# Norm statistics from token-major x in the weight stream, and four PSUM banks for the stream's sums

## The chip, the cores and the metric

The kernel runs on one core of one Trainium2 chip. A core has TensorE (PE, matrix products into PSUM), VectorE (DVE), ScalarE (ACT), GpSimd (POOL) and SyncE (SP), whose queue issues the DMAs here. PSUM has eight banks of 128 x 512 fp32 in this kernel's use. The metric is device time in microseconds (us), the median of several runs; lower is better.

## The reference

A hybrid block over x of 256 tokens and 2048 channels: a root-mean-square norm, one wide input projection, three mixers (A: state space, B: attention with selected, window and compressed keys, C: retention), a gated merge, an output projection and a gated embedding.

```python
def rms_norm(x, gain=None):
    y = x * lax.rsqrt(jnp.mean(x * x, axis=-1, keepdims=True) + EPS)
    return y * gain
...
    h = rms_norm(x, norm_pre[i])
    (xa, za, ba, ca, dta, qb, kcb, vcb, ksb, vsb, kwb, vwb, gb, zb,
     qc, kc, vc, zc, gm) = jnp.split(h @ w_in[i], offsets, axis=-1)
    ya = ssd_mixer(xa, za, ba, ca, dta, ...)
    yb = nsa_mixer(qb, kcb, vcb, ksb, vsb, kwb, vwb, gb, zb, ...)
    yc = retention_mixer(qc, kc, vc, zc, ret_norm[i])
    u = jnp.einsum('bsjw,jwd->bsjd', jnp.stack([ya, yb, yc], axis=2), w_branch[i])
    gates = jax.nn.sigmoid(gm).reshape(b, L, N_BRANCH, D_MODEL)
    x = x + rms_norm(jnp.sum(gates * u, axis=2) @ w_out[i], norm_post[i])
    g = jax.nn.sigmoid(rms_norm(x) @ ple_gate[i])
    x = x + rms_norm(g * (p[i] @ ple_proj[i]), ple_norm[i])
```

## The kernel before

All weights pass through one stream. plan (L27) lists its pieces: a chunk is 512 output columns of one weight matrix, such as ba0 or qc0, in four pieces of 1 MB each (four k-tiles of 128 rows by 512 columns). load (L187) issues a piece's DMA on SP into one of three raw buffers; split (L197) makes a high part hi on ACT (L214) and a low part lo on DVE (L215), both in the reduced format fp32r. mm_part then multiplies each k-tile with x, which is held transposed and split in the same way (xh, xl): three products hi.xh, lo.xh, hi.xl (L938, L939, L940) for each of two halves t of the tokens, so 96 matmuls of 128 x 512 a chunk. A "stream matmul" below is one of these, counted from the program's start. Their sums stand in a PSUM bank of the pool mm (mmbank, three banks), one for each chunk and half, until evac reads it. Two more pools are tp (two banks, transposes) and bg (bgbank, three banks, the products of the mixers, called the background here).

x is multiplied with norm_pre but not with its norm: the projections use raw x, and every evacuation scales by rstd, one number for each token. So no bank can be evacuated before rstd is there.

The start is written by hand: first (L234) loads x transposed (xtr, which lies in the tile yh) and the first chunk in fine pieces, and first_split (L244) makes for each k xh on ACT (L248), xl on DVE (L249), hi on ACT (L253) and lo on DVE (L254). stats (L263) squares xtr on ACT (L266, eight of 128 x 512), adds the squares on POOL (L269, seven), sums over the channels with small matmuls against ones (by Chain, L130), and rsqrt (L174) makes rstd. The piece sm (columns for dt and the gates) comes after ba0 and is multiplied in small (L296).

The background of a chunk is written after the chunk (pend, flush, after). For a key/value group g of branch B, bg_q does soft for each half of the tokens (four rounds r: scores into one or two bg banks, L600 and L603; copy L611 on ACT; mask adds L612 and L613 and maximum L616 on DVE; exps L619 on ACT; scaling L624 on DVE), then soft_cmp for the compressed keys (L632 to L652), then mix: tiles of transposes (L181), a high part on ACT (L666, tile u1) and a low part on DVE (L667, tile u2), products with the values (L130), and the copy of the result to y (L671). bg_zb then multiplies with the gate of the chunk zb and writes yh (L487, ACT) and yl (L488, DVE), from which the chunks wB are multiplied. q0 to q3 are the four groups; the chunks run q0, zb0, ... q3, zb3, gmB0, qc0, wB0.

A scheduler that works on a modelled timeline sets the order of the instructions on each engine out of what is ready, data and free buffers both. Each engine then runs its list in that order, so one waiting instruction holds up all behind it.

Of the kernel before, what the change touches and what calls it, by code (L numbers as in the profile page):

```python
# [8 lines left out]
F32 = mybir.dt.float32  # L9
# [5 lines left out]
P = 128  # L15
# [11 lines left out]
def plan():  # L27
    """The weight stream: a list of (chunk, piece); a chunk is (kind, index)."""
    s = []

    def add(kind, n):
        s.extend(((kind, n), j) for j in range(4))

# [5 lines left out]
    for kind, cnt in (("ba", 2), ("ca", 2), ("xa", 4), ("za", 4)):  # L39
        for n in range(cnt):  # L40
            add(kind, n)
            if kind == "ba" and n == 0:
                s.append((("sm", 0), 0))
# [42 lines left out]
def build(ctx, tc, I, out, LA=3, SA=2, HB=4, WARM=9):  # L86
    nc = tc.nc
    ST = plan()
    NP = len(ST)
    SM = ST.index((("sm", 0), 0))  # L90

# [21 lines left out]
    def mmbank():  # L113
        return PS("mm", [P, CH], 3)

# [3 lines left out]
    def bgbank(shape):  # L119
        return PS("bg", shape, 3)  # L120

    nodep = mybir.DependencyInfo(mybir.DependencyClass.NoSync, mybir.DependencyReason.DATA)

    class Chain:
        """Keeps the accumulation groups of one PSUM bank in trace order."""
        def __init__(self):
# [11 lines left out]

# [1 line left out]
    cst = const.tile([P, I["cst"].shape[1]], F32, name="cst")  # L140
# [27 lines left out]
    nc.vector.memset(ones, 1.0)  # L168
    # the activation tables load while the first operands are on their way
    ld = const.tile([P, 1], F32, name="ld")  # L170
    nc.scalar.activation(ld, ones, AF.Copy)

    def rsqrt(dst, src, n):
        """dst = (src / n + eps) ** -0.5"""  # L174
        w = src.shape[-1]
        t = W("rs", [P, w], 2)
        nc.vector.tensor_scalar(t, src, 1.0 / n, EPS, ALU.mult, ALU.add)
        nc.gpsimd.tensor_tensor(out=dst, in0=t, in1=mhalf.to_broadcast([P, w]), op=ALU.pow)
# [3 lines left out]

# [1 line left out]
    raw = {}  # L184
    spl = {}

    def load(s):  # L187
        if ST[s][0][0] == "sm":
            raw[s] = stream.tile([P, KT, 80], F32, name=nm("raw"), tag="raw", bufs=3)
            nc.sync.dma_start(raw[s], I["ws"])  # L190
            return
        raw[s] = stream.tile([P, 4 * CH], F32, name=nm("raw"), tag="raw", bufs=3)
        if s < 4:
            return
        nc.sync.dma_start(raw[s], I["wst"][s if s < SM else s - 1])

    def split(s):  # L197
        if ST[s][0][0] == "sm":
            hi, lo = BIG("mg", [P, 2, KT, 80], F32R), None
            hi, lo = hi[:, 0], hi[:, 1]  # L200
            nc.scalar.activation(hi, raw[s], AF.Copy)
            nc.vector.tensor_sub(lo, raw[s], hi.bitcast(F32))
            spl[s] = (hi, lo)
            del raw[s]
            return
        hs, ls = [], []
        for h in range(2):
# [4 lines left out]
            if s >= 4:  # L212
                r = raw[s][:, h * 2 * CH:(h + 1) * 2 * CH]
                nc.scalar.activation(hi, r, AF.Copy)  # L214
                nc.vector.tensor_sub(lo, r, hi.bitcast(F32))  # L215
# [3 lines left out]

# [1 line left out]
    xh = BIG("xh", [P, KT, T], F32R)  # L221
    xl = BIG("xl", [P, KT, T], F32R)
    xtr = BIG("yh", [P, KT, T])
    xsq = BIG("yl", [P, KT, T])
    ssq = BIG("y", [P, 2, T])

    # keeps the tensor engine busy, and so at its full clock, until the first operands are there
    wz = W("u1", [P, CH], 2, mybir.dt.bfloat16)
# [5 lines left out]
    def first(q):  # L234
        """k-tiles 4q..4q+3 of x and of the first chunk's weights, loaded and split finely"""
        load(q)
# [26 lines left out]
    def stats():  # L263
        """rstd per token from the transposed x, and the tables of scales that hang on it"""
        for k in range(0, KT, 2):
            nc.scalar.activation(xsq[:, k:k + 2, :], xtr[:, k:k + 2, :], AF.Square)  # L266
            if k == 0:
                continue
            nc.gpsimd.tensor_tensor(out=ssq, in0=xsq[:, 0:2, :] if k == 2 else ssq, in1=xsq[:, k:k + 2, :], op=ALU.add)  # L269
        ps = bgbank([P, 2])  # L270
        ch = Chain()
        for t in range(2):
            for i in range(2):
                ch.mm(ps[:, t:t + 1], ssq[:, i, t * P:(t + 1) * P], ones, i == 0, i == 1)
        rsqrt(rstd, ps, D)
        # tables of scales per token for branches B and C
        nc.vector.tensor_scalar_mul(rsc, rstd, 128.0 ** -0.5)
# [5 lines left out]
    rk = [rstd[:, t:t + 1] for t in range(2)]  # L283
# [1 line left out]
    sg = const.tile([P, 2, 48], F32, name="sg")  # L285
# [6 lines left out]
    def small(wsh, wsl):  # L292
# [19 lines left out]
        nc.scalar.activation(ea, V.alog, AF.Exp)  # L312
        # log(1 + e) = 2 atanh(e / (2 + e)), by its series: (e / (2 + e)) ** 2 is at most 1 / 9
        z = W("dtz", [P, 2, 32], 1)
# [21 lines left out]

# [1 line left out]
    S = K()  # L338
# [7 lines left out]
    def to_T(rows, pair):  # L346
        """rows: the tokens' tile per half; pair of 128-column blocks -> PSUM [128, 2, 256]"""
        tp = tpbank([P, 2, T])
# [5 lines left out]

# [1 line left out]
    def conv(rows, ct0, dest):  # L356
# [37 lines left out]
    def bg_xa(n):  # L394
# [20 lines left out]
        nc.gpsimd.tensor_tensor(out=xe, in0=xdt[0], in1=bc(dend[:, hsl]), op=ALU.mult)  # L415
        # the state after the first chunk
        st = bgbank([P, CH])
# [31 lines left out]

# [1 line left out]
    def ev_z(ps, n, t):  # L451
# [51 lines left out]

# [44 lines left out]
    def bg_cmpout(i, ps):  # L548
# [9 lines left out]
        if i == 0:  # L558
# [6 lines left out]
            return  # L565
        # rows 0..15, 16..31 and 32..47: [high, high, low], for [high, low, high] of the other operand
        h3 = W("u4", [P, 2, 4, 3, 16], 2)
# [10 lines left out]
    def bg_q(g):  # L578
# [49 lines left out]
        def soft_cmp(t, ss):  # L628
            sgt = sg[:, t, :].rearrange("p (h b) -> p h b", b=3)
            # compressed keys  # L630
            mx = W("mx", [P, 4], 2)
# [45 lines left out]

# [1 line left out]
    def ev_rot(ps, kind, n, t):  # L679
# [56 lines left out]

# [1 line left out]
    def ev_w(ps, br, n, t):  # L738
# [31 lines left out]

# [1 line left out]
    def ev_wo(ps, n, t):  # L772
# [74 lines left out]
    def ev_pg(ps, n, t, half=None):  # L847
        """half: of the columns of the last chunk, whose last token half comes in two parts"""
        c0, w = (n * CH, CH) if half is None else (n * CH + half * 256, 256)
# [20 lines left out]

# [1 line left out]
    def evac(ch, ps, t):  # L872
# [50 lines left out]

    acc = {}

    def mm_part(ch, j, t, hs, ls, half=None):
        """the products of piece j of a chunk for half t of the tokens (and half of the columns)"""
        H, L = lhs(ch[0])
# [12 lines left out]
        if j == 3:  # L941
            if half is None:
                evac(ch, ps, t)
            else:
                ev_pg(ps, ch[1], t, half)
            del acc[key]
# [15 lines left out]
    for q in range(4):  # L962
        first(q)
    nc.sync.dma_start(cst, I["cst"])
    nc.sync.dma_start(vec, I["vec"])
    done = [4, 4]
    pend = []

    def ahead(s):
        while done[0] <= min(s + LA, NP - 1):  # L970
            load(done[0])
            done[0] += 1
            while done[1] <= min(s + SA, done[0] - 1):
                split(done[1])
                done[1] += 1
        while done[1] <= min(s + SA, NP - 1):
            split(done[1])
            done[1] += 1
# [6 lines left out]
    while s < NP:  # L985
        ch, j = ST[s]
        two = (ch == ("wo", 3) and j == 2) or (ch == ("pg", 0) and j == 0) or (ch == ("pg", 3) and j == 2)
        if s < 4:
            first_split(s)
            if s == 1:  # L990
                stats()
        ahead(s)
        if ch[0] == "cmp":
            flush()
# [20 lines left out]
        del spl[s]  # L1015
        if j == 3:
            pend.append(ch)
        s += 1


# [1 line left out]
CST = [("ident", (P,)), ("tri", (P,)), ("stri", (P,)), ("cos", (2, P)), ("sin", (2, P)),  # L1022
# [37 lines left out]
def layout(inputs):  # L1060
# [9 lines left out]
    def block(w):  # L1070
        """[2048, 512] -> 4 pieces [128, 4 * 512]"""
        return w.reshape(4, 4, P, CH).transpose(0, 2, 1, 3).reshape(4, P, 4 * CH)
# [18 lines left out]
    ST = plan()  # L1091
    ST.remove((("sm", 0), 0))
    wst = np.empty((len(ST), P, 4 * CH), np.float32)
# [47 lines left out]
```

## Time and profile before

| | |
|---|---|
| median of 3 runs | 1828.5 us (1827.67 to 1828.92) |
| span of the profiled execution | 1826.8 us |
| PE busy | 1809.6 us (99%) |
| DVE busy | 1080.0 us (59%) |
| ACT busy | 950.5 us (52%) |
| POOL busy | 176.7 us (10%) |
| bytes moved by DMA | 333.72 MB, 183 GB/s in the mean |

The page gives no time of the profiled execution other than its span. Busy time is the sum over an engine's instructions without overlap. A PE row's duration (about 0.39 us for 128 x 512) is the time from its start to its end, and the next one starts earlier, since matmuls are pipelined; what a matmul costs PE is the step from one start to the next. In a timeline the brackets give the idle time of the engine before an instruction and what ended it.

### The profile page before, as it was taken

The page shows a single profiled execution, that of the slowest core. Times are in us where ns is not written, and L with a number is a line of the kernel's source. Part 1 is how long each engine was busy: PE and PEld are TensorE (multiplying, and loading weights), DVE is VectorE, ACT ScalarE, POOL GpSimd, SP SyncE. Part 2 cuts the span into 40 slices and gives each one's busy share as a digit, 9 for nine tenths or more (in the row PEclk, how much of TensorE's full clock was granted, in tenths as well). Part 3 has the DMA queues.
Part 4 walks back from the last instruction along what each step waited for, and adds up shares of the span by engine and source line. Part 5 has one row for each costly group of instructions (what it writes and reads, how often), then busy time and mean ns, then how long its engine had stood idle before and what let it go on. Part 6 is the DMA issues. An engine that isn't in the chain of part 4 may idle for free.

```text
span 1826.8 us, 21792 instructions
## 1 busy us (share of the span) xinstructions
PE 1809.6 (99%) x8531; PEld 1502.2 (82%) x8531; DVE 1080.0 (59%) x1453; ACT 950.5 (52%) x1264; POOL 176.7 (10%) x167
## 2 busy tenths in 40 slices
PE   8999999999999999999999999999999999999997
PEld 6888888888888888888878888888888888888886
DVE  7666876544457547667674545655656544555665
ACT  6656566544346547656754444344445544444653
POOL 2001340000022000000011011102110000110001
PEclk9999999999999999999999999999999999999999
DMA  7443434555556654344435555445454555565653
GB/s 284 164 182 139 152 141 176 184 192 199 185 183 254 232 194 151 139 161 147 149 144 196 196 186 205 162 165 189 170 207 175 184 188 203 185 230 186 228 185 116
DMA packets 49496, 333.72 MB, mean 183 GB/s; under 512 B 5617, under 2 KB 6385, under 8 KB 10225
## 3 DMA queue, kind: packets, MB, share of 16 engines
q1 hardware_dynamic: 48960, 331.67, 50.3%
q8 instruction: 67, 1.10, 0.2%
q10 hardware_dynamic: 432, 0.66, 0.1%
q14 instruction: 37, 0.30, 0.0%
HBM read 330.21 MB, written 2.10 MB: 182 GB/s over the span
## 4 chain that ended last, share of the span: by engine, by line
PE 95%; ACT 2%; DVE 1%; issue 1%; POOL 0%; DMA 0%; SPq 0%; POOLq 0%; ACTq 0%; DVEq 0%
PE mm L939 28%; PE mm L940 28%; PE mm L938 28%; PE tp L181 3%; PE bg L130 2%; PE bg L137 1%; PE bg L600 1%; PE bg L957 1%; DVE lo L215 0%; PE bg L433 0%; DMA raw<-wst 0%; ACT hi L214 0%; PE mm L844 0%; PE mm L296 0%; POOL u L540 0%
## 5 line engine op out<-in xcount | busy, mean ns | idle before, releaser
L215 DVE TENSOR_TENSOR lo<-raw,hi 128x1024 fp32r<-128x1024 f32 x604 | 745.0, 1237 | 596.0 <-ACT hi L214 573.6
L214 ACT ACTIVATE hi<-raw 128x1024 fp32r<-128x1024 f32 x604 | 637.8, 1060 | 644.0 <-PE mm L940 623.6
L939 PE MATMUL mm<-lo,xh 128*128 128x512 f32 x1856 | 727.0, 393 | 3.6 <-DVE lo L254 3.1
L940 PE MATMUL mm<-hi,xl 128*128 128x512 f32 x1856 | 725.0, 392 | 0.0
L938 PE MATMUL mm<-hi,xh 128*128 128x512 f32 x1856 | 719.9, 392 | 0.5 <-ACT hi L253 0.5
L939 PEld LDWEIGHTS mm<-lo,xh 128*128 128x128 f32 x1856 | 348.9, 188 | 77.3 <-DVE lo L254 6.1
L938 PEld LDWEIGHTS mm<-hi,xh 128*128 128x128 f32 x1856 | 348.3, 188 | 72.1 <-ACT hi L253 1.7
L940 PEld LDWEIGHTS mm<-hi,xl 128*128 128x128 f32 x1856 | 348.8, 188 | 69.8 <-issue 0.2
L939 PE MATMUL mm<-lo,yh 128*128 128x512 f32 x496 | 193.6, 390 | 0.0
L940 PE MATMUL mm<-hi,yl 128*128 128x512 f32 x496 | 193.1, 390 | 0.0
L938 PE MATMUL mm<-hi,yh 128*128 128x512 f32 x496 | 192.6, 390 | 0.0
L940 PEld LDWEIGHTS mm<-hi,yl 128*128 128x128 f32 x496 | 93.1, 188 | 19.2
L938 PEld LDWEIGHTS mm<-hi,yh 128*128 128x128 f32 x496 | 93.1, 188 | 19.2
L939 PEld LDWEIGHTS mm<-lo,yh 128*128 128x128 f32 x496 | 93.1, 188 | 18.9
L748 POOL TENSOR_TENSOR mg<-mg,u 128x512 f32<-128x512 f32 x16 | 27.9, 1745 | 372.0 <-DVE u L747 372.0
L430 POOL TENSOR_TENSOR u<-ahl,cst 128x512 fp32r<-128x512 f32 x32 | 43.5, 1373 | 92.9 <-PE bg L433 62.4
L366 DVE SCALAR_TENSOR_TENSOR u<-tp,vec,u 128x255 f32<-128x255 f32 (+2 forms) x96 | 41.0, 473 | 5.0 <-ACT u L362 4.6
L540 POOL TENSOR_TENSOR u<-gate,vec 128x120 f32<-128x120 f32 x32 | 21.9, 723 | 212.4 <-ACT gate L516 211.2
L647 POOL COPY pc<-pch 128x64 f32<-128x64 f32 x8 | 5.7, 715 | 341.8 <-ACT pch L644 341.8
L619 ACT ACTIVATE u<-u,nmx 128x128 f32<-128x128 f32 (+1 forms) x64 | 28.5, 446 | 6.4 <-DVE nmx L616 2.9
L181 PE MATMUL tp<-cst,u 128*128 128x128 f32 (+1 forms) x194 | 30.1, 273 | 0.8 <-ACT u L368 0.8
L690 POOL TENSOR_TENSOR u<-u,u 128x256 f32<-128x256 f32 x16 | 18.6, 1162 | 112.0 <-DVE u L688 94.6
(236 smaller groups left out, 1208.2 us busy)
## 6 DMA issues: line engine op xcount, KB each, us to landing
raw<-wst SPq DMA_DIRECT2D x302, 1024.0 KB, 4.8
raw<-wst SPq DMA_DIRECT2D x6, 512.0 KB, 8.6
y<-xn SPq DMA_DIRECT2D x2, 1024.0 KB, 5.9
xl<-plen SPq DMA_DIRECT2D x2, 1024.0 KB, 5.0
yh<-xT SPq DMA_DIRECT2D x6, 256.0 KB, 8.5
out_dram<-xh SPq DMA_DIRECT2D x4, 352.0 KB, 2.4
raw<-wst SPq DMA_DIRECT2D x4, 256.0 KB, 4.4
u<-npost SPq DMA_DIRECT2D x4, 256.0 KB, 4.8
```

Of the source, the lines that this page charges most:

```text
L130: i = nc.tensor.matmul(o, lhsT, rhs, start=start, stop=stop)
L181: nc.tensor.transpose(dst, src, ident[0:k, 0:k])
L214: nc.scalar.activation(hi, r, AF.Copy)
L215: nc.vector.tensor_sub(lo, r, hi.bitcast(F32))
L366: nc.vector.scalar_tensor_tensor(cv[:, jj, sh:], tp[:, jj, :T - sh], V.cw[:, ct, j:j + 1], cv[:, jj, sh:], ALU.mult, ALU.add)
L430: nc.gpsimd.tensor_tensor(out=asg, in0=ahl[:, i, c, 4 * g:4 * g + 4].bitcast(F32).unsqueeze(2).to_broadcast([P, 4, P]), in1=CP.tri.unsquee ...
L540: nc.gpsimd.tensor_tensor(out=bf[:, :, g, :], in0=src[:, g], in1=V.pe[:, i, l0:l0 + 8].unsqueeze(2).to_broadcast([P, 8, 15]), op=ALU.add)
L619: nc.scalar.activation(pr_[:, b, :], pr_[:, b, :], AF.Exp, bias=nmx[:, b:b + 1], accum_out=sm2[:, b:b + 1])
L748: nc.gpsimd.tensor_tensor(out=S.mg[:, t, sl], in0=S.mg[:, t, sl], in1=tmp, op=ALU.add)
L938: nc.tensor.matmul(ps, H[:, kk, tsl], wh, start=(kk == 0), stop=False)
L939: nc.tensor.matmul(ps, H[:, kk, tsl], wl, start=False, stop=False)
L940: nc.tensor.matmul(ps, L[:, kk, tsl], wh, start=False, stop=(kk == KT - 1))
```

## The change

- stats no longer uses xtr. Two pieces of token-major x, ("xn", 0) and ("xn", 1), 1 MB each, stand in the stream after the second and third piece of ba1. split squares each on ACT as one 128 x 2048 activation with the sum accumulated into a column of ssx, and after the second one rsqrt makes rstd from ssx. The squares of xtr, the POOL adds and the small matmuls are gone.
- The two sums of ba0 stay in their banks (late) until then; they are evacuated and ba0's background is queued after the second piece.
- The piece sm moves from behind ba0 to behind ba1; its split parts lie in the tile yh.
- mmbank has four banks, bgbank two.
- The two DMAs of the tables cst and vec are issued behind the load of stream piece 4, and ahead (the look-ahead of loads and splits) does not split beyond piece 3 in the first three steps.
- Comments and docstrings are blanked; line numbers shift by 5 to 19, by 10 in mm_part, by 9 in the background.

```diff
     def add(kind, n):
-        s.extend(((kind, n), j) for j in range(4))
+        for j in range(4):
+            s.append(((kind, n), j))
+
+            if (kind, n) == ("ba", 1) and j in (1, 2):
+                s.append((("xn", j - 1), 0))
...
-            if kind == "ba" and n == 0:
+            if kind == "ba" and n == 1:
                 s.append((("sm", 0), 0))
...
     def mmbank():
-        return PS("mm", [P, CH], 3)
+        return PS("mm", [P, CH], 4)
...
     def bgbank(shape):
-        return PS("bg", shape, 3)
+        return PS("bg", shape, 2)
...
     def split(s):
+        if ST[s][0][0] == "xn":
+            t = ST[s][0][1]
+            nc.scalar.activation(xj, raw[s], AF.Square, accum_out=ssx[:, t:t + 1])
+            spl[s] = None
+            del raw[s]
+            if t == 1:
+                stats()
+                for ev in late:
+                    evac(*ev)
+                pend.append(("ba", 0))
+            return
...
     def stats():
-        for k in range(0, KT, 2):
-            nc.scalar.activation(xsq[:, k:k + 2, :], xtr[:, k:k + 2, :], AF.Square)
-            if k == 0:
-                continue
-            nc.gpsimd.tensor_tensor(out=ssq, in0=xsq[:, 0:2, :] if k == 2 else ssq, in1=xsq[:, k:k + 2, :], op=ALU.add)
-        ps = bgbank([P, 2])
-        ch = Chain()
-        for t in range(2):
-            for i in range(2):
-                ch.mm(ps[:, t:t + 1], ssq[:, i, t * P:(t + 1) * P], ones, i == 0, i == 1)
-        rsqrt(rstd, ps, D)
+        rsqrt(rstd, ssx, D)
...
         if j == 3:
-            if half is None:
+            if ch == ("ba", 0):
+                late.append((ch, ps, t))
+            elif half is None:
                 evac(ch, ps, t)
...
-    nc.sync.dma_start(cst, I["cst"])
-    nc.sync.dma_start(vec, I["vec"])
...
             load(done[0])
+            if done[0] == 5:
+                with tc.issue_after(getattr(dma[0], "ins", dma[0])):
+                    nc.sync.dma_start(cst, I["cst"])
+                    nc.sync.dma_start(vec, I["vec"])
             done[0] += 1
-            while done[1] <= min(s + SA, done[0] - 1):
+            while done[1] <= min(s + SA if s > 2 else 3, done[0] - 1):
                 split(done[1])
...
             first_split(s)
-            if s == 1:
-                stats()
```

How the order moves, at three places. First ACT in the start, the rows that follow the table load; xh and hi are the split of x and of the weights, and the tile yl of the row with L266 holds squares. Before:

```order
L248 ACTIVATE xh_80<-yh_82,npre 128x256 [waits DMAHW1_49,DMAHW0_49]
L253 ACTIVATE hi_134<-raw_108 128x512 [waits DMAHW2_49]
L248 ACTIVATE xh_80<-yh_82,npre 128x256 [waits DMAHW3_49]
L266 ACTIVATE yl_83<-yh_82 128x512
L253 ACTIVATE hi_134<-raw_108 128x512 [waits DMAHW4_49]
L248 ACTIVATE xh_80<-yh_82,npre 128x256 [waits DMAHW5_49]
L253 ACTIVATE hi_136<-raw_108 128x512 [waits DMAHW6_49]
L248 ACTIVATE xh_80<-yh_82,npre 128x256 [waits DMAHW7_49]
L266 ACTIVATE yl_83<-yh_82 128x512
```

After:

```order
L267 ACTIVATE xh_80<-yh_82,npre 128x256 [waits DMAHW1_49,DMAHW0_49]
L272 ACTIVATE hi_132<-raw_108 128x512 [waits DMAHW2_49]
L267 ACTIVATE xh_80<-yh_82,npre 128x256 [waits DMAHW3_49]
L272 ACTIVATE hi_132<-raw_108 128x512 [waits DMAHW4_49]
L267 ACTIVATE xh_80<-yh_82,npre 128x256 [waits DMAHW5_49]
L272 ACTIVATE hi_134<-raw_108 128x512 [waits DMAHW6_49]
L267 ACTIVATE xh_80<-yh_82,npre 128x256 [waits DMAHW7_49]
```

The squares have gone, and the splits of x and of the weights follow each other.

Second PE at the border of the chunks gmB0 and qc0, around the first matmul of qc0 (mm_7623 before, mm_7609 after); bg, tp, u and ev belong to the mix of q2 and to the background of zb2. Before:

```order
L938 MATMUL mm_7494<-hi_7513,xh_80 128x512
L939 MATMUL mm_7494<-lo_7514,xh_80 128x512
L940 MATMUL mm_7494<-hi_7513,xl_81 128x512
L938 MATMUL mm_7623<-hi_7543,xh_80 128x512 [waits Activation_49]
L939 MATMUL mm_7623<-lo_7544,xh_80 128x512 [waits DVE_49]
L940 MATMUL mm_7623<-hi_7543,xl_81 128x512
```

After:

```order
L135 MATMUL bg_6672<-u_1244_6714,yl_4735 128x512 [waits Activation_49]
L135 MATMUL bg_6672<-u_1245_6715,yl_4735 128x512 [waits DVE_49]
L135 MATMUL bg_6672<-u_1244_6714,yl_4735 128x512
L135 MATMUL bg_6672<-u_1232_6670,vc_847_4797 128x512
L186 MATMUL tp_6871<-cst,ev_6826 128x128 [waits PE_49]
L186 MATMUL tp_6871<-cst,ev_6840 128x128
L186 MATMUL tp_6871<-cst,ev_6826 128x128
L186 MATMUL tp_6871<-cst,ev_6840 128x128
L948 MATMUL mm_7609<-hi_7529,xh_80 128x512 [waits Activation_49]
```

Before, the first matmul of qc0 follows the last ones of gmB0 directly; after, the second half of q2's mix (33 rows of transposes and products ahead of qc0, of which the last eight are printed) stands between the two chunks.

Third PE around the first matmuls of wB0, which read yh (mm_7779 before, mm_7765 and mm_7778 after); bg rows with u1 and u2 of L130 and L135 are mix products, those of L612 scores of soft, tp rows transposes of the softmaxed scores. Before:

```order
L940 MATMUL mm_7636<-hi_7655,xl_81 128x512
L938 MATMUL mm_7779<-hi_7685,yh_7476 128x512
L939 MATMUL mm_7779<-lo_7686,yh_7476 128x512
L130 MATMUL bg_7271<-u_1361_7289,yl_4749 128x512 [waits Activation_49]
L130 MATMUL bg_7271<-u_1362_7290,yl_4749 128x512 [waits DVE_49]
L130 MATMUL bg_7271<-u_1361_7289,yl_4749 128x512
L181 MATMUL tp_7308<-cst,u_1319_7122 128x128 [waits PE_49]
L181 MATMUL tp_7308<-cst,u_1324_7143 128x128
```

After:

```order
L612 MATMUL bg_7164<-yh_4487,gate_7019 128x256 [waits DVE_49]
L612 MATMUL bg_7164<-yh_4487,gate_7019 128x256
L612 MATMUL bg_7164<-yh_4487,u_1298_7021 128x256
L948 MATMUL mm_7765<-hi_7671,yh_7462 128x512 [waits Activation_49]
L949 MATMUL mm_7765<-lo_7672,yh_7462 128x512
L948 MATMUL mm_7778<-hi_7671,yh_7462 128x512
L949 MATMUL mm_7778<-lo_7672,yh_7462 128x512
L135 MATMUL bg_7207<-u_1345_7213,yl_4735 128x512 [waits DVE_49]
L135 MATMUL bg_7207<-u_1346_7214,yl_4735 128x512
L135 MATMUL bg_7207<-u_1345_7213,yl_4735 128x512
```

Before, the first matmuls of wB0 stand behind q3's second to last mix tiles, with three tiles to go; after, they stand directly behind the last round of q3's soft, with both calls of mix and the second soft_cmp still to go.

## Rows read from the trace of the kernel before

**Rows 1.** The page, part 1: each engine's busy time, share of the span and instructions.

```profile
PE 1809.6 (99%) x8531; PEld 1502.2 (82%) x8531; DVE 1080.0 (59%) x1453; ACT 950.5 (52%) x1264; POOL 176.7 (10%) x167
```

**Rows 2.** Stretches: us, busy PE, PEld, DVE, ACT, POOL (count), PEclk, DMA share, GB/s.

```profile
10.00:20.00 10.00, 7.28 (x28) 4.72 (x28) 9.09 (x11) 9.83 (x22) 6.68 (x5) 1.00 1.03 384
34.61:1817.00 1782.39, 1779.77 (x8419) 1482.03 (x8417) 1048.76 (x1403) 923.13 (x1211) 161.61 (x152) 1.00 0.50 181
887.60:938.35 50.75, 49.72 (x250) 40.60 (x248) 36.31 (x96) 39.12 (x76) 1.91 (x4) 1.00 0.41 147
1820.00:1823.00 3.00, 0.00 (x0) 0.00 (x0) 2.42 (x2) 1.01 (x2) 2.33 (x3) 0.50 0.31 120
```

**Rows 3.** Timeline of PE, start: start, duration, instruction, [idle before, releaser].

```profile
5.14 1.22 PE L938 MATMUL mm<-hi,xh 128*128 128x512 f32 x2
...
10.91 0.74 PE L938 MATMUL mm<-hi,xh 128*128 128x512 f32 x2 [0.46 <-ACT hi L253]
...
25.78 0.50 PE L939 MATMUL mm<-lo,xh 128*128 128x512 f32 x1 [0.78 <-DVE lo L254]
...
28.67 0.39 PE L939 MATMUL mm<-lo,xh 128*128 128x512 f32 x1
...
30.94 0.62 PE L938 MATMUL mm<-hi,xh 128*128 128x512 f32 x2
31.39 0.95 PE L130 MATMUL bg<-ones,y 128*128 128x1 f32 x8
...
34.61 0.28 PE L296 MATMUL mm<-xh,mg 128*80 128x256 f32 x1
```

**Rows 4.** Timeline of DVE and of ACT in the start.

```profile
14.98 2.96 DVE L249 SCALAR_TENSOR_TENSOR xl<-yh,npre,xh 128x256 fp32r<-128x256 f32 x2
...
26.25 0.87 DVE L249 SCALAR_TENSOR_TENSOR xl<-yh,npre,xh 128x256 fp32r<-128x256 f32 x2
27.04 1.28 DVE L254 TENSOR_TENSOR lo<-raw,hi 128x512 fp32r<-128x512 f32 x2
...
21.69 1.14 ACT L253 ACTIVATE hi<-raw 128x512 fp32r<-128x512 f32 x2
```

**Rows 5.** Lines from 5 to 35 us: group, count | busy, mean ns | idle before, releaser.

```profile
L254 DVE TENSOR_TENSOR lo<-raw,hi 128x512 fp32r<-128x512 f32 x16 | 12.9, 832 | 3.1 <-ACT hi L253 3.0
...
L269 POOL TENSOR_TENSOR y<-y,yl 128x512 f32<-128x512 f32 x6 | 8.7, 1445 | 4.8 <-ACT yl L266 4.6
```

**Rows 6.** Timeline of PE and of DVE at the end of q3.

```profile
935.02 0.60 PE L181 MATMUL tp<-cst,u 128*128 128x128 f32 x4
935.38 0.94 PE L130 MATMUL bg<-u,yl 128*128 128x512 f32 x3
...
937.68 0.73 PE L130 MATMUL bg<-u,yl 128*128 128x512 f32 x2 [0.69 <-DVE u L667]
...
938.72 3.69 DVE L488 TENSOR_TENSOR yl<-y,yh 128x512 fp32r<-128x512 f32 x6
```

**Rows 7.** Lines from 880 to 940 us, columns as in rows 5.

```profile
L214 ACT ACTIVATE hi<-raw 128x1024 fp32r<-128x1024 f32 x17 | 17.8, 1053 | 6.6 <-PE mm L940 5.5 <-ACT u L666 0.9
...
L667 DVE TENSOR_TENSOR u<-tp,u 128x512 fp32r<-128x512 f32 x6 | 4.1, 687 | 2.9 <-ACT u L666 2.9
...
L619 ACT ACTIVATE u<-u,nmx 128x256 f32<-128x256 f32 x8 | 4.0, 499 | 0.2 <-DVE sm L621 0.2
L619 ACT ACT_TABLE_LOAD x3 | 3.8, 1283 | 0.0
...
L666 ACT ACTIVATE u<-tp 128x512 fp32r<-128x512 f32 x6 | 3.6, 593 | 3.9 <-PE tp L181 3.9
...
L487 ACT ACTIVATE yh<-y 128x512 fp32r<-128x512 f32 x6 | 3.2, 628 | 0.0
...
L616 DVE TENSOR_REDUCE nmx<-u 128x2 f32<-128x512 f32 x4 | 2.7, 681 | 0.0
...
L646 POOL COPY pc<-pch 128x64 f32<-128x64 f32 x2 | 1.4, 704 | 1.3 <-DVE pc L645 1.3
```

More of the change, by code (lines that the diff above doesn't have):

```diff
@@ L89, in build @@
     NP = len(ST)
-    SM = ST.index((("sm", 0), 0))
+    WI = [sum(c[0] not in ("sm", "xn") for c, _ in ST[:i]) for i in range(NP)]
     const = ctx.enter_context(tc.tile_pool(name="const", bufs=1))
@@ L185, in build @@
     spl = {}
+    dma = [None]
     def load(s):
@@ L194, in load @@
             return
-        nc.sync.dma_start(raw[s], I["wst"][s if s < SM else s - 1])
+        dma[0] = nc.sync.dma_start(raw[s], I["xn"][ST[s][0][1]] if ST[s][0][0] == "xn" else I["wst"][WI[s]])
     def split(s):
+        if ST[s][0][0] == "xn":
[9 more added lines that the diff above has]
+            return
         if ST[s][0][0] == "sm":
-            hi, lo = BIG("mg", [P, 2, KT, 80], F32R), None
+            hi, lo = BIG("yh", [P, 2, KT, 80], F32R), None
             hi, lo = hi[:, 0], hi[:, 1]
@@ L213, in split @@
                 r = raw[s][:, h * 2 * CH:(h + 1) * 2 * CH]
-                nc.scalar.activation(hi, r, AF.Copy)
+                i = nc.scalar.activation(hi, r, AF.Copy)
+                if s == 4:
+                    tc.keep_in_program_order(i)
                 nc.vector.tensor_sub(lo, r, hi.bitcast(F32))
@@ L223, in build @@
     xtr = BIG("yh", [P, KT, T])
-    xsq = BIG("yl", [P, KT, T])
-    ssq = BIG("y", [P, 2, T])
+    xj = BIG("yl", [P, D])
+    ssx = const.tile([P, 2], F32, name="ssx")
     wz = W("u1", [P, CH], 2, mybir.dt.bfloat16)
@@ L924, in build @@
     acc = {}
+    late = []
     def mm_part(ch, j, t, hs, ls, half=None):
@@ L971, in ahead @@
             load(done[0])
+            if done[0] == 5:
+                with tc.issue_after(getattr(dma[0], "ins", dma[0])):
+                    nc.sync.dma_start(cst, I["cst"])
+                    nc.sync.dma_start(vec, I["vec"])
             done[0] += 1
-            while done[1] <= min(s + SA, done[0] - 1):
+            while done[1] <= min(s + SA if s > 2 else 3, done[0] - 1):
                 split(done[1])
                 done[1] += 1
-        while done[1] <= min(s + SA, NP - 1):
+        while done[1] <= min(s + SA if s > 2 else 3, NP - 1):
             split(done[1])
@@ L989, in build @@
             first_split(s)
-            if s == 1:
-                stats()
         ahead(s)
-        if ch[0] == "cmp":
+        if ch[0] == "xn":
+            pass
+        elif ch[0] == "cmp":
             flush()
@@ L1015, in build @@
         del spl[s]
-        if j == 3:
+        if j == 3 and ch != ("ba", 0):
             pend.append(ch)
@@ L1091, in layout @@
     ST = plan()
-    ST.remove((("sm", 0), 0))
+    ST = [c for c in ST if c[0][0] not in ("sm", "xn")]
     wst = np.empty((len(ST), P, 4 * CH), np.float32)
```

## The prediction

> **What bounds the kernel now.** First the engines' shares: TensorE (PE) is busy 1809.6 us, 99% of the span; VectorE (DVE) is at 59%, ScalarE (ACT) at 52% [rows 1]. A change can therefore save only PE work or PE's gaps, and loses wherever it opens a gap. Next the stretches, to see where the gaps are. PE runs 7.28 of the ten microseconds from 10 to 20; in the 50.75 us of the last key/value group's attention (called q3 below) it runs 49.72; from 34.61 to 1817 it has 2.6 us of gaps in all; at the end it stands still, and its granted clock is 0.50 there [rows 2]. So there are two places to work out: the start, where there is something to win, and q3, where PE is almost without a gap and could get some.
>
> **The start.** Chunk ba0 is 96 matmuls. The row starts at 28.67 and 30.94, with nine between, give ten steps in 2.27 us, 0.227 each, so ba0 needs 21.9 us. It ran from 5.14 to 34.61 = 29.5 us with 0.95 us of statistics matmuls inside [rows 3]: 6.7 us are stalls or the half-rate first matmuls. Each k needs 6 matmuls (1.37 us). DVE should not be behind: its clean pair L249 takes 0.87 and its clean pair L254 1.28 for two k, 1.08 us for one; but while GpSimd (POOL) adds squares, the pair L249 took 2.96 [rows 4], and L254 is 832 ns in the mean of the stage [rows 5]. PE waits for this lo, as in the 0.78 us at 25.78 [rows 3]. The change removes the POOL adds L269 (six of 1445 ns and a first one), and the eight squares L266 from ACT, which then keeps up too: its two weight casts for two k take 1.14 us [rows 4], and the two smaller casts of x no more than that, so at most 1.14 for one k.
>
> In the Trainium skill, "SBUF — State Buffer", section "Who interferes with whom", a VectorE instruction with two SBUF inputs and a GpSimd instruction that reads SBUF take turns at one port, and the loser waits for the whole instruction. The trace agrees: 2.96 beside 0.87 us. By that rule the whole stretch goes with the adds; without it, only the ACT time would.
>
> 18 matmuls had started before the one at 10.91 [rows 3]; until then weights are arriving, and from 10 to 20 us the DMA runs at a share of 1.03 and 384 GB/s [rows 2], so nothing is won earlier. From there 78 x 0.228 = 17.8 us plus, as an estimate, 0.8 us of waits in the first two k: ba0 ends at 29.5 and not at 34.6. **Gain 5.1 us**, at least 3.5 (another 1.6 us of waits where weights land late), at most 6.5 (all the gaps). The two ACT squares of 128x2048 that come in are between two and two and a half 128x1024 casts each: 2.0 to 2.6 us, from an engine that is half idle; ba0's kept banks are then evacuated some 3 us ahead of the matmul that needs one, by the same durations. The 2 MB more are 5 to 8 us of transfer, spread over ba1's 22 us: I take nothing; 0 to 2 us is the bound. The later place of the small piece "sm" moves one 128x1280 cast pair and five matmuls: nothing. The two table transfers that are issued later are needed after ba0 only: nothing.
>
> **The banks.** The stream gets a fourth bank, the background keeps two of three, and the scheduler's order changes all along. The stream has hardly a bank wait to lose: outside the start and the end, PE's gaps are 2.6 us in all, and 1.0 of them lies in q3 [rows 2]. With two banks the background chain runs later against the stream. At q3 that becomes visible, since chunk wB0 reads its result. In the old order q3's soft starts at stream matmul 3301 and at 3458 only three mix tiles are left, which cost one wait of 0.69 us [rows 6]. In the new order the soft of q3 starts at 3399, and all that can go ahead without it ends at 3460.
>
> First place (before qc0): 20 transposes, 12 mix products and a value product stand alone on PE, with no stream matmul between them; the first matmul of qc0 then waits for a bank that ACT evacuates only after these tiles. From the last gmB0 matmul: ACT first does a hi cast (1.05); three tiles end at 5.6 (each 0.59 ACT, then 0.69 DVE [rows 7], with other casts and a transpose between); value product, copy and table load (1.28 [rows 7]) to 8.3, evacuation to 9.0. A transpose takes PE 0.0875 us (the four at 935.02 end with the product at 935.38 [rows 6]), a 512-column product as much as a stream matmul: 20 x 0.0875 + 12 x 0.23 + 0.25 = 4.8 us of work. **Loss 4.3 us**, 0 to 6: nothing if ACT and DVE have run ahead of PE by the tiles, 6 if the table load also comes late.
>
> Second place (wB0): after the last free qc0 matmul, the second half's soft rounds r1 to r3, mix(0), the compressed keys and mix(1) follow, with four stream matmuls in all. In microseconds from there: the rounds end at 7.9. With two banks a round cannot start before DVE has read the one before; each has two PE groups of three half-width matmuls (0.36 us each), a copy on ACT, an add and a maximum on DVE (0.68 the latter), and ACT has two exps of 0.50 of the last round between [rows 7]: 2.6 in series. Six casts yh in a row on ACT (3.2 [rows 7]) stand ahead of the last exps: 11.1. Exps of r2 and r3, 1.0 each, and the compressed one: 13.4. Weights, their POOL copy (0.7 [rows 7]) and rounding: 16.0; transposes: 16.7. Four mix tiles, the first 1.6, then 1.1 each by ACT's and DVE's halves: 21.7. Value product, last transposes: 22.8. DVE's masks and the first yl (3.69 for six [rows 6]): 24.0, and the stream goes on. PE's own work in it: 18 soft matmuls x 0.12, 40 transposes x 0.0875, 20 products x 0.23, 4 x 0.228 = 11.2 us. **Loss 12.8 us.** The lower bound is 8: the casts yh and the first exps (4.3 us) may have been done by an ACT that is ahead. The upper bound is 15: the spare second bank costs a further DVE wait per round. I take the middle since the old q3 shows DVE and ACT together as the chain (36.31 and 39.12 us busy of 50.75 [rows 2]) and not ahead.
>
> Elsewhere the order moves by a few instructions: the gaps of q0 to q2 and of the xa chunks may grow or go, 0 to 3 us; I take nothing. The 1.0 us of gaps that q3 has now is part of the stalls counted above and goes.
>
> **Sum.** The profiled execution's span is 1826.8 us; the median of the runs shown is 1828.5, so 1.7 us lie around the span. 1826.8 - 5.1 + 4.3 + 12.8 - 1.0 = 1837.8 us of span, 1839.5 with what lies around it.
>
> **Rivals.** A, faster: the banks cost nothing. If ACT and DVE run far enough ahead of PE, both chains are covered, and only the start is left: 1828.5 - 5.1 = 1823.4. For it: q3 is covered now, with one 0.69 us wait. Against it: it now has 157 stream matmuls (36 us) from its start, then 61 (14 us). It decides at a chain under about 14 us of stream plus 14 us of its own PE work; the steps above sum to 39 us from the soft's start. Chance 0.12. In between, half the losses hidden: 1828.5 - 5.1 - 1.0 + 8.5 = 1830.9, within 0.2%, 0.08.
>
> B, slower by more: the start gives nothing, because 10 to 20 us is a stage of full DMA [rows 2] and PE then waits for weights where it waited for lo. 1839.5 + 5.1 = 1844.6. Against it: PE's wait in the row ends on lo [rows 3], and lo is late while POOL adds [rows 4]. Chance 0.10.
>
> C, slower by more: TensorE's clock. After PE's last work, at 1817, the granted clock is 0.50 (1.2 GHz) from 1820 on, where it was 1.00 (2.4 GHz) before [rows 2]. In the second place PE would have 2.5 us of work in the 8 us of casts and exps. If the clock falls there, the products and transposes behind it cost double where they are in the chain (3 us), and the first stream matmuls after it run at half pace, as the first two of the kernel do (1.22 us for the two, beside 0.39 for one later [rows 3]); +4 us: 1843.5. Chance 0.15. The Trainium skill, "TensorE: Matmul & The Clock Gate", section "HAM oscillation — how this bites in real kernels", tells the same of matmuls in bursts between waits: each burst starts at half clock. By that rule rival C is the likelier case; the trace has idle PE only at its ends, so I don't take it.
>
> **How the numbers follow.** The forecast with its own spread (1833 to 1843) has 0.55, A 0.12, the half 0.08, B 0.10, C 0.15. A measurement of this kernel can tell about 0.2%, 3.7 us, from no change. Faster by more than that: 0.12; within: 0.08; slower: 0.80. The range leaves out A and the far end of B and C: 1826 to 1846.
>
> **What would show it.** The start: ba0's last matmul near 29.5, L254 (now L273) near 0.68 us throughout, no POOL adds. The first place: a gap of PE near 4 us before the first matmul of qc0, ended by ACT's evacuation. The second: some 13 us of PE gaps before the first product with yl, ended by DVE and ACT. Wrong would be a PE that stays busy in both, or granted clocks at 0.5 in the middle of the span.

## Result and profile after

| | before | after |
|---|---|---|
| median of 5 runs | 1828.5 us | 1838.74 us (1837.54 to 1840.15) |
| span of the profiled execution | 1826.8 us | 1835.7 us |
| PE busy | 1809.6 us | 1812.7 us |

The changed kernel is slower: the ratio is 1.0057, with a 95% interval of 1.0045 to 1.0069. 1839.5 was forecast. The page of the changed kernel, its span, part 1 and the engines of the chain:

```profile
span 1835.7 us, 21743 instructions
...
PE 1812.7 (99%) x8523; PEld 1504.7 (82%) x8523; DVE 1073.2 (58%) x1453; ACT 946.9 (52%) x1257; POOL 160.9 (9%) x160
...
PE 95%; DVE 2%; ACT 2%; issue 0%; POOL 0%; DMA 0%; SPq 0%; POOLq 0%; ACTq 0%; DVEq 0%
```

PE is still the bound (compare [rows 1]). It has 23.0 us without work where it had 17.2, and is busy 3.1 us longer although the statistics matmuls are gone. Where the time goes is seen best if one counts stream matmuls and compares when the same one starts. This table is worked out from the timelines of PE, minus the time in the kernel before (negative is earlier). Its figures are good to some 0.3 us, since the timelines merge neighbouring rows; the experiments below are in it already:

```
stream matmul     before    after  E1    E2    E3    E4    E5    E6    E7    E8
95 (end of ba0)     34.4    -6.0  -5.7  -0.5    *    +0.1  -3.6  +1.4  -5.9  -5.4
480                136.3    -4.7  -5.7  -0.5  -0.2  -2.3  -3.6  +1.4  +3.3  -5.4
2400 (before q0)   635.4    -4.8  -5.6  -0.5  -0.2  +0.8  -3.4  +1.2  +3.2  -5.3
3552 (after wB0)   961.4    +9.9  -5.5 +12.7 +15.1 +45.6  -3.4  +1.1  +3.3  -5.2
6624               1691.6  +10.0  -5.3 +12.7 +15.1 +46.7  -3.4  +1.3  +3.5  -5.0
7040               1807.7   +8.7  -5.3 +11.4 +15.1 +48.3  -3.4  +1.3  +3.5  -5.6
* counted in another order there
```

So the changed kernel wins 6.0 us in ba0, of which 4.7 are left at matmul 480, loses 14.7 between the matmuls 2400 and 3552, and wins 1.3 more near 1720 us.

**The start.** The timeline of PE in the start, with the first matmul of ba0, the one after which it runs on without a pause, and the last of ba0; then DVE's two groups from 5 to 35 us:

```profile
5.25 1.10 PE L948 MATMUL mm<-hi,xh 128*128 128x512 f32 x2
...
11.93 0.73 PE L948 MATMUL mm<-hi,xh 128*128 128x512 f32 x2
...
28.42 0.39 PE L950 MATMUL mm<-hi,xl 128*128 128x512 f32 x1
```

```profile
L273 DVE TENSOR_TENSOR lo<-raw,hi 128x512 fp32r<-128x512 f32 x16 | 10.5, 689 | 3.1 <-ACT hi L272 3.0
L268 DVE SCALAR_TENSOR_TENSOR xl<-yh,npre,xh 128x256 fp32r<-128x256 f32 x15 | 6.7, 479 | 0.0
```

Ba0's last matmul starts at 28.42, 6.0 us earlier. DVE's lo takes 689 ns where it took 832 [rows 5], its xl 479, about half the pair of 0.87 us that ran beside no add [rows 4]. Then ACT, with the two squares of the new pieces and the kept evacuations of ba0:

```profile
31.71 1.92 ACT L206 ACTIVATE yl<-raw 128x2048 f32<-128x2048 f32 x1 [1.56 <-DMA raw<-xn]
...
36.71 1.92 ACT L206 ACTIVATE yl<-raw 128x2048 f32<-128x2048 f32 x1 [0.44 <-DMA raw<-xn]
...
39.75 1.27 ACT L352 ACTIVATE ev<-mm,rstd 128x512 f32<-128x512 f32 x2 [1.03 <-POOL rstd L183]
```

The squares cost 1.92 us each and stand in ACT's idle time; the evacuations run from 39.75, and PE has no wait there.

**The waits of PE that are new.** The groups of waits, total, count, longest:

```profile
PE tp L186 <- POOL pc L655: 4.1, 1, 4.1
PE mm L948 <- ACT ev L903: 2.1, 1, 2.1
...
PE bg L135 <- DVE u L676: 1.1, 2, 0.9
PE bg L142 <- ACT eacs L344: 0.9, 1, 0.9
```

**The border of gmB0 and qc0.** PE, from the last matmul of gmB0 to qc0, and ACT ahead of it:

```profile
889.72 0.40 PE L950 MATMUL mm<-hi,xl 128*128 128x512 f32 x1
...
899.85 0.50 PE L948 MATMUL mm<-hi,xh 128*128 128x512 f32 x1 [2.10 <-ACT ev L903]
...
900.88 0.63 PE L948 MATMUL mm<-hi,xh 128*128 128x512 f32 x1
901.31 0.63 PE L949 MATMUL mm<-lo,xh 128*128 128x512 f32 x1
...
903.83 0.40 PE L949 MATMUL mm<-lo,xh 128*128 128x512 f32 x1
904.07 0.39 PE L950 MATMUL mm<-hi,xl 128*128 128x512 f32 x1
```

```profile
897.20 0.60 ACT L680 ACTIVATE y<-bg 128x512 f32<-128x512 f32 x1 [1.98 <-PE bg L135]
897.81 1.28 ACT L903 ACT_TABLE_LOAD   x1
899.11 1.27 ACT L903 ACTIVATE ev<-mm,rstd 128x512 f32<-128x512 f32 x2
```

The last matmul of gmB0 starts at 889.72, the first of qc0 at 899.85, 10.1 us later; PE waits 2.10 us at the end for an evacuation that stands behind the copy of y and a table load; ahead of that it waits twice for DVE's u, 1.1 us together. Then look at the steps: from 900.88 to 901.31 it is 0.43 us, from 903.83 on 0.24. The stretches say why, and show the same a second time after the wait at 940 (columns as in rows 2):

```profile
10.00:20.00 10.00, 10.00 (x43) 7.73 (x42) 9.22 (x19) 9.03 (x20) 0.00 (x0) 1.00 1.03 396
900.00:904.00 4.00, 4.00 (x11) 3.17 (x12) 0.00 (x0) 0.37 (x1) 0.00 (x0) 0.57 0.02 4
936.00:940.00 4.00, 0.42 (x1) 0.11 (x1) 2.52 (x14) 2.82 (x11) 0.07 (x1) 1.00 0.00 0
940.00:944.00 4.00, 3.37 (x15) 2.56 (x16) 1.26 (x3) 1.73 (x3) 0.43 (x2) 0.66 0.01 2
944.00:948.00 4.00, 3.97 (x22) 3.06 (x20) 2.14 (x5) 1.20 (x2) 0.00 (x0) 0.91 0.00 0
```

The granted clock is 0.57 from 900 to 904, 0.66 from 940 to 944 and 0.91 from 944 to 948: PE stood, and then the clock was at its lower level, 1.2 GHz, for a while. A mean of 0.57 over 4 us is 3.4 us at half clock, and the other two come to 3.4 us together. The first stretch, 10 to 20, has PE busy throughout.

**The wait of wB0.** PE from the last free matmul of qc0 to the first product with yl, and ACT in between:

```profile
926.36 0.39 PE L950 MATMUL mm<-hi,xl 128*128 128x512 f32 x1
...
932.42 0.28 PE L612 MATMUL bg<-yh,u 128*128 128x256 f32 x1
...
940.48 0.62 PE L186 MATMUL tp<-cst,pc 128*48 128x128 f32 x4 [4.06 <-POOL pc L655]
...
949.72 0.49 PE L950 MATMUL mm<-hi,yl 128*128 128x512 f32 x1 [0.41 <-DVE yl L497]
```

```profile
932.73 3.23 ACT L496 ACTIVATE yh<-y 128x512 fp32r<-128x512 f32 x6
...
937.34 0.50 ACT L628 ACTIVATE u<-u,nmx 128x256 f32<-128x256 f32 x1
...
937.84 0.24 ACT L643 ACTIVATE ss<-ss 128x64 f32<-128x64 f32 x1
```

23.4 us lie between the starts of the last free matmul (926.36) and the first product with yl (949.72); in them PE starts four stream matmuls. The six casts yh stand on ACT ahead of the last exps, and PE's longest wait, 4.06 us, ends on POOL's copy behind these.

### The profile page after: what moved, and what is told of

It is laid out like the page before. It is cut to its first block, busy times and chain, and to the rows that moved or that the text cites. A ratio compares the mean times of both kernels' runs of the same rounds, so it can differ in the third digit from the quotient of the medians.

```text
span 1835.7 us, 21743 instructions
## 1 busy us (share of the span) xinstructions
PE 1812.7 (99%) x8523; PEld 1504.7 (82%) x8523; DVE 1073.2 (58%) x1453; ACT 946.9 (52%) x1257; POOL 160.9 (9%) x160
## 4 chain that ended last, share of the span: by engine, by line
PE 95%; DVE 2%; ACT 2%; issue 0%; POOL 0%; DMA 0%; SPq 0%; POOLq 0%; ACTq 0%; DVEq 0%
PE mm L949 29%; PE mm L950 29%; PE mm L948 28%; PE tp L186 3%; PE bg L135 2%; PE bg L142 1%; DVE lo L234 1%; PE bg L969 1%; PE mm L853 1%; PE bg L609 1%; DVE u L375 0%; ACT hi L231 0%; PE bg L442 0%; PE mm L305 0%; POOL u L549 0%
## 5 line engine op out<-in xcount | busy, mean ns | idle before, releaser
L186 PEld LDWEIGHTS tp<-cst,u 128*128 128x128 f32 (+1 forms) x194 | 24.5, 144 | 6.5 <-ACT u L377 1.1
```

What stands on the lines that cost most here:

```text
L186: nc.tensor.transpose(dst, src, ident[0:k, 0:k])
```

## Experiments

In the table above E1 to E8 are the experiments in this order.

**E1, the start alone.**

```diff
-        return PS("mm", [P, CH], 4)
+        return PS("mm", [P, CH], 3)
...
-        return PS("bg", shape, 2)
+        return PS("bg", shape, 3)
...
-            acc[key] = mmbank() if half is None else bgbank([P, 256])
+            acc[key] = bgbank([P, CH]) if (ch, t) == (("ba", 1), 1) else mmbank() if half is None else bgbank([P, 256])
```

> The changed kernel with three stream banks and three background banks again; the one bank too few in the start (the second half of chunk ba1) is taken from the background's pool, which is idle there. On PE the order from q0 to wB0 has q3's soft at stream matmul 3301 and its last value product at 3458, as before the change. Theory (start wins 4.7 us, the banks lose 14.7 us): the gain of the start stays and the loss goes, 1828.5 - 4.7 = 1823.8 us, between 1822.5 and 1825.5. Rival (the loss hangs on the moved statistics or the longer stream, not on the banks): about 1838 us. A gap of PE of 3 us or more at 890 to 950 would speak for the rival.

Measured 1823.7 us (1823.18 to 1824.21), against 1828.64 for the kernel before on the same chip: ratio 0.9973, 0.9963 to 0.9984. PE's longest waits in it:

```profile
PE bg L251 <- DVE ss L800: 1.2, 1, 1.2
PE tp L186 <- ACT u L377: 0.8, 1, 0.8
PE bg L135 <- DVE u L676: 0.7, 1, 0.7
```

They are those of the kernel before; the new ones of the changed kernel are gone. The change of the statistics is a gain, and the whole loss hangs on the banks (and on the order that the scheduler makes of them). This version is faster than both kernels.

**E2, the banks alone.** The kernel before with four stream banks and two background banks.

> The kernel before with four stream banks and two background banks, nothing else. On PE the order from q0 to wB0 is that of the changed kernel (soft of q3 at 3399, last value product at 3460). Theory: all of the loss and none of the gain, 1828.5 + 14.7 - 1.2 (a gain in the last 120 us that the changed kernel shows) = 1842 us, between 1839 and 1845, with the start as before (first matmul of the second chunk at 41 us). Rival (the loss hangs on the start or the stream): 1828 us.

Measured 1841.93 us (1840.31 to 1842.81), ratio 1.0071, 1.0058 to 1.0085. In the table the loss is 13.2 us at the attention, and the gain of 1.3 us near 1720 is there as well. The order there is that of the changed kernel, whose loss was 14.7. The difference is about what the clock explains. Stretches of E2's profiled execution, around the border of gmB0 and qc0 and behind the wait of wB0:

```profile
900.00:904.00 4.00, 1.78 (x8) 0.90 (x7) 1.49 (x3) 2.50 (x4) 0.00 (x0) 1.00 0.27 109
904.00:908.00 4.00, 3.88 (x17) 3.21 (x18) 0.00 (x0) 0.64 (x2) 0.00 (x0) 1.00 0.00 0
...
944.00:948.00 4.00, 4.00 (x17) 2.80 (x16) 1.39 (x2) 1.90 (x4) 0.00 (x0) 0.61 0.00 0
```

After the same waits (E2 is later by 4.3 us there, and its wait for the evacuation is 2.1 us too) the clock here stays at 1.00 at the border and falls only at wB0, 0.61. So the same PE order does not always bring the clock down; one fall is worth about 1.5 us here, and half of the changed kernel's 3.4 us at half clock is 1.7.

**E3, two background banks.** The kernel before with `PS("bg", shape, 2)`, still three for the stream.

> The kernel before with two background banks and still three for the stream; one PSUM bank is unused. It tells which half of the bank change loses. On PE q3's soft starts at stream matmul 3329 and all value products but one are done at 3458. Theory as predicted (two background banks make the chain late): a loss of the same kind, +8 to +15 us, 1837 to 1843 us. Rival (the fourth stream bank lets the stream run ahead of the background): 28 matmuls (6.4 us) later than before only, of which the old order has little slack, so +1 to +6 us, 1829.5 to 1834.5.

Measured 1843.01 us (1842.27 to 1843.98), ratio 1.0079, 1.0065 to 1.0092: at the upper end of what the theory said. PE's longest new waits:

```profile
PE mm L938 <- ACT ev L894: 4.2, 2, 2.1
...
PE tp L181 <- POOL pc L646: 3.1, 1, 3.1
```

They are of the same two kinds, an evacuation behind a late mix (at two borders here, near 826 and 892 us) and the POOL copy. Its own order has the soft of q3 70 stream matmuls earlier than the changed kernel, and it loses as much: the position of the soft in the order, by which the rival was priced, does not tell the loss. Two banks are enough to cause it. Not all of the loss is waiting: in this trace the clock is at half for 13.7 us in three falls, where the changed kernel has 6.8 in two.

**E4, four stream banks.** The kernel before with `PS("mm", [P, CH], 4)` and `PS("tp", shape, 1)`.

> The kernel before with four stream banks and still three for the background; the transposes have one bank for two. On PE q3's soft starts at 3401 and its last value product stands at 3460, close to the changed kernel. Theory as predicted (two background banks make the chain late): with three of them the chain is short of transposes' banks only, +0 to +6 us, up to 1834.5. Rival (the fourth stream bank): a loss like the changed kernel's at q3, +12 us or more, 1840 us or more, with PE's gaps on ACT and DVE between the last matmul of qc0 and wB0.

Measured 1878.0 us (1877.17 to 1879.61), ratio 1.0271, 1.0257 to 1.0285. Its longest waits are others:

```profile
PE bg L130 <- ACT u L666: 9.3, 13, 1.0
PE tp L181 <- ACT u L652: 3.8, 3, 2.4
```

With one transposes' bank mix tiles wait for ACT's read of the one before (13 waits behind u of L666). The time is far off the theory, which said 1834.5 at most. PE's idle time is 39.4 us against 17.2 in the kernel before, 22 us more, and the mean granted clock is 0.985 against 0.998: for 48 us of its trace the clock is at half, so up to 24 of the 49 us lost can be the clock's. The number would suit the rival, but the waits point to the missing transposes' bank, so this experiment does not tell what a fourth stream bank does by itself. That is read from E3 and E2: with two background banks, the version with the fourth stream bank is 1.1 us the faster in the median (in the table 15.1 against 11.4, but E3's trace is of its slowest run and E2's of its fastest). A loss by the fourth bank is not seen.

**E5, no adds.**

```diff
-            nc.gpsimd.tensor_tensor(out=ssq, in0=xsq[:, 0:2, :] if k == 2 else ssq, in1=xsq[:, k:k + 2, :], op=ALU.add)
...
-                ch.mm(ps[:, t:t + 1], ssq[:, i, t * P:(t + 1) * P], ones, i == 0, i == 1)
+                ch.mm(ps[:, t:t + 1], xsq[:, 14 + i, t * P:(t + 1) * P], ones, i == 0, i == 1)
```

> The kernel before without the seven POOL adds of squares; the eight squares on ACT stay, and the small matmuls sum one pair of k-tiles only, so the statistics are not those of the reference. Theory (DVE's lo is late because POOL's adds hold it up): nearly all of the start's gain, ba0's last matmul 3.5 to 4.7 us earlier than 34.4, 1824 to 1825.5 us, and lo near 0.68 us throughout. Rival (ACT, which also carries the squares, is the late engine): less than 1.5 us, 1827 us or more.

Measured 1824.02 us (1823.52 to 1825.06), ratio 0.9977, 0.9968 to 0.9986. DVE's groups from 5 to 35 us:

```profile
L254 DVE TENSOR_TENSOR lo<-raw,hi 128x512 fp32r<-128x512 f32 x16 | 10.5, 690 | 3.5 <-ACT hi L253 3.4
L249 DVE SCALAR_TENSOR_TENSOR xl<-yh,npre,xh 128x256 fp32r<-128x256 f32 x15 | 6.7, 482 | 1.7 <-ACT xh L248 1.2
```

They are as in the changed kernel (689 and 479 ns), with the squares still on ACT. PE has one wait in ba0:

```profile
PE mm L937 <- ACT hi L253: 1.3, 1, 1.3
```

So the adds are 3.6 of the 6.0 us that the changed kernel wins in ba0. Of the other 2.4 us, this wait on ACT, which still squares, is 1.3, and the statistics matmuls, which are still there, take 0.95 [rows 3].

**E6, no squares.**

```diff
         for k in range(0, KT, 2):
-            nc.scalar.activation(xsq[:, k:k + 2, :], xtr[:, k:k + 2, :], AF.Square)
             if k == 0:
+                nc.scalar.activation(xsq[:, k:k + 2, :], xtr[:, k:k + 2, :], AF.Square)
                 continue
-            nc.gpsimd.tensor_tensor(out=ssq, in0=xsq[:, 0:2, :] if k == 2 else ssq, in1=xsq[:, k:k + 2, :], op=ALU.add)
+            nc.gpsimd.tensor_tensor(out=ssq, in0=xsq[:, 0:2, :] if k == 2 else ssq, in1=xsq[:, 0:2, :], op=ALU.add)
```

> The kernel before with one square on ACT instead of eight; the seven POOL adds stay and add that one tile again and again, so the statistics are not those of the reference. Theory (POOL's adds): little is won, less than 1.5 us, 1827 us or more, since lo stays as late while the adds run; they now run in a row, from about 6 us to 17, and leave the second half of ba0 free, so not slower either. Rival (ACT's squares): 3 us or more, 1825.5 us or less.

Measured 1829.98 us (1828.31 to 1830.15), ratio 1.0007, 0.9998 to 1.0016: nothing is won. DVE's groups, and POOL's adds:

```profile
L254 DVE TENSOR_TENSOR lo<-raw,hi 128x512 fp32r<-128x512 f32 x16 | 13.0, 843 | 1.4 <-ACT hi L253 1.4
L249 DVE SCALAR_TENSOR_TENSOR xl<-yh,npre,xh 128x256 fp32r<-128x256 f32 x15 | 10.8, 748 | 0.0
```

```profile
7.29 9.26 POOL L269 TENSOR_TENSOR y<-y,yl 128x512 f32<-128x512 f32 x6
```

The adds now run in a row from 7.29 to 16.55, and DVE is as slow as in the kernel before. E5 and E6 together show the main cause of the start's stalls: POOL's adds; ACT's load has the smaller share that E5 shows. In the trace ba0 ends 1.4 us later, where "not slower" was expected. PE's waits, and the stretch behind the last of them (columns as in rows 2):

```profile
PE mm L939 <- DVE lo L254: 4.7, 4, 1.8
```

```profile
18.00:22.00 4.00, 4.00 (x12) 3.09 (x12) 4.00 (x10) 2.25 (x6) 0.00 (x0) 0.57 1.03 406
```

The waits for lo are 4.7 us where they were 3.1, now all in the first half of ba0, and behind them the clock is at half for 3.4 us, which costs 1.7; part of this is made up in the second half, where no add runs. The clock also parts the runs: three of the ten, with a mean granted clock of 0.998 or 0.999, took 1828.3 to 1828.7 us, as the kernel before; the seven with 0.997 took 1829.8 to 1830.2.

**E7, three banks without borrowing.** E1 without its last edit.

> The changed kernel with three stream banks and three background banks, without the borrowed one. Ba0's two sums keep their banks until the second piece of x has been squared, near 40 us, so one half of ba1 has no bank. Theory (this is what the fourth bank is for): PE does the first half of ba1's first two pieces (24 matmuls, 5.5 us from 28.7), then waits to about 40 us; the loss is 5 to 8 us against the version with the borrowed bank, 1829 to 1832 us. Rival (the order finds other work): within 1.5 us of 1823.7.

Measured 1832.69 us (1830.83 to 1834.24), ratio 1.0024, 1.0014 to 1.0034; against E1 9.0 us, one more than the 8 expected at most. PE's longest wait, and the stretch behind it:

```profile
PE mm L948 <- ACT ev L352: 6.4, 1, 6.4
```

```profile
40.00:45.00 5.00, 4.25 (x10) 3.41 (x11) 1.47 (x6) 3.34 (x4) 0.00 (x0) 0.50 0.33 125
```

The wait of 6.4 us is the one expected; the clock is 0.50 from 40 to 45, after it, which the expectation had not counted. The wait and half of those 5 us are 8.9 us, and the table has 9.2 (from -5.9 to +3.3). So the start does need a fourth bank, but for 24 us only: in E1 the borrowed bank is in use from 29.2 to 53.1 us.

**E8, borrowing twice.** E1, and in the embedding product mm_pp the sums of the second token half in the background's pool:

```diff
-                ps = mmbank()
+                ps = bgbank([P, CH]) if t else mmbank()
```

> The version that is fastest so far (three and three banks, one half of ba1 in a background bank), and in the embedding product near the end the sums of the second token half in background banks as well. The changed kernel won 1.2 us near 1720 us, where this product runs; with the banks as before that gain is not there. Theory (it came from the number of banks for these eight sums): 1823.7 - 1.2 = 1822.5 us. Rival (it came from the order around it): 1823.7 us.

Measured 1823.18 us (1822.69 to 1823.5), ratio 0.9971, 0.9961 to 0.9982. E1 and E8 ran on different occasions, and 0.5 us between them is less than either interval tells; in the table the part behind matmul 6624 is 0.6 us shorter. Whether the 1.3 us came from these banks stays open.

## Why the prediction was right

The time came 0.8 us beside the forecast; the direction, the cause in the start and the two places of the loss were right. That it came so near is in part luck. Against the span of the trace, which is of the fastest of the five runs, the forecast was 2.1 us too long (1837.8 for 1835.7). And in the loss two errors cancelled: PE waits less than forecast, and works longer.

- **The start, gain 5.1.** 6.0 at the end of ba0, 4.7 after the first background: right within its bounds (3.5 to 6.5). The estimated 0.8 us of waits in the first two k did not come; then 1.3 is given back, 0.9 of it a new wait of a background product (L142) on ACT's eacs, which I had priced at nothing. E1, with three background banks again, keeps 5.3 to 5.7. That the adds are the main cause is shown by E5 and E6: in E6 DVE's two groups are 843 and 748 ns beside the adds, in E5 690 and 482 without. By the Trainium skill, "SBUF — State Buffer", section "Who interferes with whom", such a VectorE instruction and a GpSimd instruction that reads SBUF contend; these numbers agree, though no run here shows the port itself.
- **Nothing for the 2 MB, the squares, sm and the tables.** Right: PE has no wait from 10 to 100 us.
- **First place, loss 4.3.** The chain from the last gmB0 matmul to qc0 took 10.1 us where the steps summed to 9.0; the three tiles and the value product were longer by that. Less the 4.8 us of work that were summed, the loss would be 5.3 (9.0 less 4.8 is 4.2, not 4.3), and some 1.7 more where the clock falls. But PE is idle for only 3.3 us of it, and 2.10 of these end with the evacuation, where the sign named was a gap near 4 us.
- **Second place, loss 12.8.** The chain took 23.1 us behind the last free matmul, where 24.0 was summed: rounds 6.1 (7.9 summed), casts to 9.4 (11.1), exps to 11.5 (13.4), transposes from 13.9 (16.0); then the four tiles and the rest took 9.2 where 8.0 was summed, with the granted clock at 0.66 and 0.91. Less the 11.2 us of work that were summed, the loss would be 11.9. The sign named was some 13 us of PE's gaps; they are 6.8 us, and the longest, 4.06, ends on POOL's copy behind the casts and exps.
- **Both places together.** 17.1 less the 1.0 of gaps that were there, 16.1 us, was forecast; the table has 14.7 between matmuls 2400 and 3552. Between their starts PE has the same 1580 matmuls in both kernels. That stretch before, then after, then the two places after (columns as in rows 2):

```profile
635.19:961.13 325.94, 324.91 (x1581) 268.14 (x1580) 209.65 (x446) 203.11 (x353) 16.92 (x21) 1.00 0.43 155
```

```profile
630.62:971.22 340.60, 330.51 (x1582) 271.14 (x1581) 215.23 (x446) 198.38 (x348) 11.74 (x21) 0.99 0.41 149
889.72:899.85 10.13, 6.80 (x36) 4.46 (x34) 5.62 (x7) 5.50 (x9) 0.00 (x0) 1.00 0.33 123
926.58:949.72 23.14, 16.38 (x84) 11.83 (x82) 16.07 (x48) 15.14 (x39) 2.39 (x5) 0.93 0.23 89
```

PE is idle for 1.0 us before and 10.1 after, and these 10.1 are the 3.3 and 6.8 of the two places. So the rest of the attention has no gap in either kernel, as I had assumed, but idle time is only 9.1 of the 14.7 us. The clock stands at half for 6.8 us, which costs up to 3.4. The remaining 2.2 or more are PE's own steps, which take longer between waits than in a full stream. The mis-sized term is PE's own work: 4.8 and 11.2 us were summed at the steps of a full stream, and PE was busy 6.8 and 16.4.
- **Rival C** (the clock) was partly true. "Granted clocks at 0.5 in the middle of the span" was named as a sign of being wrong, and it came. I set it apart as another case with 4 us; it is a part of the likeliest one, and costs some 1.7 us at the border (1.5 by E2 beside the changed kernel) and, as an estimate from the 9.2 for 8.0 above, about 1 us at wB0. By the Trainium skill, "TensorE: Matmul & The Clock Gate", section "HAM oscillation — how this bites in real kernels", the bursts of a matmul kernel between its waits start at half clock; the rows at 900 and 940 agree, the one of E2 at 904 does not, after a wait as long as that at 900.
- **Rival A and B** did not happen: the gaps are there, and the start gave what it should.
- **The end.** 1.3 us are won near 1720 us with four stream banks (E2 has it, E3 does not). This I did not see.
- What served the sum was to follow the order row by row and price the chain by its steps on ACT and DVE: the two chains came within 1.1 and 0.9 us of it. The words "with two banks the chain runs later" are borne out by E3; how much later, in stream matmuls, was not a measure of the loss. Each experiment changes the banks and with them the order that the scheduler makes; whether another order on two banks would do without the loss was not tried.

## What to carry to other kernels

When a resource is needed for one short stage only, borrow it there from a pool that is idle in that stage; moving it for the whole kernel moved a chain that had just been hidden into the open, and turned a gain of 5 us into a loss of 10. Where a kernel's bounding engine is full, price a change of buffers by the chains that must be ready at a fixed point of the stream, from the new order, step by step. Before blaming an engine's load for late operands, look at its durations: DVE's lo was late because each instruction took longer, not because there were too many. And where a change opens gaps on PE, count the clock with them: here 6.8 us at half clock came with 9.1 us of new gaps.

## What the runs showed of the hardware

While POOL added tiles from SBUF, DVE's instructions with two inputs from SBUF took longer: xl 748 ns in the mean (E6) beside 482 without adds (E5), lo 843 beside 690, and one pair of xl 2.96 us beside 0.87 [rows 4], though neither engine needs the other's result.

After 10.1 us in which PE was busy for 6.80, with a wait of 2.10 us at their end, the granted clock fell to half in one execution (0.57 of 900 to 904); in one of another kernel with the same PE order there it stayed at 1.00 (E2, 904 to 908). So a kernel with such gaps scatters more: the changed kernel's five runs lie 2.6 us apart, with a mean granted clock of 0.996 in the two fastest and 0.994 in the two slowest, and the eight of E1 lie 1.0 us apart. What in an execution decides it is not shown here.
